# Two layers of attention: the transposes of normed heads and keys, issued 3, 4 and 2 steps later

## The chip, the cores and the metric
One core of a Trainium2 chip. The metric is the device time of one execution in microseconds (us). The kernel before takes 1375.31 us, the median of three runs (1373.74, 1375.31 and 1376.59).

## The reference
The program is a stack of three layers over 256 tokens of width 1024, in float32. The first (windowed attention beside a state-space layer, and a large product-key expert layer behind them) is not touched. The change lies in the last two, of which the reference is, in short:

```python
def even_layer(x, ...):
    h = rmsnorm(x, ln)
    aq, ak, av, az, bq, bk, bv, bz = split_cols(h @ w_in, EVEN_SPLITS)      # 8 x 512 columns
    oa = dilated_attention(rmsnorm(aq), rmsnorm(ak), av, slopes)            # 8 heads of 64
    ob = diff_attention(rmsnorm(bq), rmsnorm(bk), bv, lam, slopes)          # 4 pairs of heads
    return x + concat([oa * silu(az), rmsnorm(ob) * silu(bz)]) @ w_out

def odd_layer(x, ...):
    h = rmsnorm(x, ln)
    cq, ck, cv, cz, dq, dkc, dvc, dks, dvs, dkw, dvw, dz, dg = split_cols(h @ w_in, ODD_SPLITS)
    oc = moba_attention(rmsnorm(cq), rmsnorm(ck), cv, slopes)
    k_cmp = rmsnorm(compress_blocks(dkc, ...))
    v_cmp = compress_blocks(dvc, ...)
    od = nsa_attention(rmsnorm(dq), k_cmp, v_cmp, rmsnorm(dks), dvs, rmsnorm(dkw), dvw, sigmoid(dg), slopes)
    return x + concat([oc * silu(cz), od * silu(dz)]) @ w_out
```

Each `rmsnorm` of a query or key works on one head of 64 values. At 256 tokens both attentions of a layer are causal and see all earlier tokens of their bands.

## The kernel before
Tokens lie on the 128 partitions, in two halves (`th` = 0, 1). `Layer.enter` transposes the input into `xH` and `xL`, a float32 number split into a rounded part and the rest. A projection is a `group`: 512 output columns, two PSUM banks (one a half, of four banks with the tag `pr`), and eight chunks `k` of the 1024 inputs. For one chunk and one half `mm3` issues three matmuls (L1702 to L1704). So a step, one chunk for both halves, is six matmuls of 512 columns.

The weights come through `Feed`: a DMA of SyncE brings a unit of 128x1024 (two chunks), ScalarE rounds it to `H` (L102), and VectorE or GpSimd subtracts to get `Lo` (L103). In these layers of three units in a row GpSimd takes two and VectorE one. Units are cut three, later four, ahead of their use.

The order of the work is written by two generators. The background yields after each step of the projections; the foreground holds the attention and says how much background it lets by (`yield STEP`) or which mark it has to wait for (`yield "bk"`). `Flow.later(n, fn)` has `fn` issued after n further yields of the background. The order of the groups, eight steps each, is bq, bk, bv, aq, ak, av, bz, az in the even layer, and raw (the keys and values to be compressed and selected), windows (280 columns), dq, cq, ck, cv, dz, cz in the odd one. Eight steps of the output projection stand behind them, so the background has 72 steps. The framework's scheduler may slip ready instructions of the projections between those of the foreground.

At the end of a query or key group `Layer.heads` squares the result on ScalarE (L1192), reduces it on VectorE (L1193), takes an inverse root by thirteen small operations on VectorE (`rstd`, L1712 to L1720) and multiplies (L1196, L1197) into the buffers `qs`, of which there are four. Then it asks for `turn`: eight transposes on TensorE (L1203) into the PSUM banks with the tag `m` (three), copied out by ScalarE (L1206) or, where a gain is applied (bq, aq, cq), by VectorE (L1208), and a mark for the foreground. `windows` does the same for two keys: squares on GpSimd (L1469), one reduction (L1470), `rstd`, four products into `kn` (L1475), and the transposes of `kn` into `kT` (L1482), with the mark `kT`. On that mark the foreground starts `compress` (L1602 on), whose last part norms the compressed key `kr` (L1630) and transposes it (L1639) behind two steps of background. Scores follow (L1295, L1298), then the weights times the values (`weigh`, L1334 and L1340).

The last attention of a layer waits for the mark `az` (`cz`) of the eighth group ahead of its second half, and the output projection for `mixed01`, which the gate `bz` (`dz`) of the seventh group leads to.

Of the kernel before, what the change touches and what calls it, by code (L numbers as in the profile page):

```python
# [1106 lines left out]
def by_head(t):  # L1107
    return t.rearrange("p (h d) -> p h d", h=8)
# [6 lines left out]
STEP = 1280  # L1115
# [3 lines left out]
class Layer(Flow):  # L1119
# [63 lines left out]
    def heads(self, t, g, scale, mark):  # L1183

        c, nc, r = self.c, self.nc, self.r
        V = nc.vector

        def done(ps):
            ss = c.small.tile([128, 16], FT, tag="hss", name="hss")
            qs = [self.pool.tile([128, 512], FT, tag="qs", name="qs", bufs=4) for _ in range(2)]  # L1190
            for th in range(2):
                nc.scalar.activation(qs[th], ps[th], AF.Square, scale=r[:, th:th + 1])  # L1192
                V.tensor_reduce(ss[:, 8 * th:8 * th + 8], by_head(qs[th]), axis=AX.X, op=OP.add)  # L1193
            rr = c.rstd(ss, 16, 1.0 / 64)
            for th in range(2):
                V.tensor_scalar(ss[:, 8 * th:8 * th + 8], rr[:, 8 * th:8 * th + 8], r[:, th:th + 1], None, op0=OP.mult)  # L1196
                V.tensor_tensor(by_head(qs[th]), by_head(ps[th]), ss[:, 8 * th:8 * th + 8, None].to_broadcast([128, 8, 64]), op=OP.mult)  # L1197

            def turn():
                for th in range(2):  # L1200
                    p = c.psum("m")
                    for k in range(4):
                        nc.tensor.transpose(p[:, k * 128:(k + 1) * 128], qs[th][:, k * 128:(k + 1) * 128], c.ident)  # L1203
                    src, dst = p.rearrange("p (k t) -> p k t", k=4), t[:, :, th * 128:(th + 1) * 128]
                    if g is None:
                        nc.scalar.activation(dst, src, AF.Copy, scale=scale)  # L1206
                    else:
                        V.tensor_scalar(dst, src, g, scale, op0=OP.mult, op1=OP.mult)  # L1208
                self.mark(mark)
            self.later(5, turn)  # L1210
        return done

    def values(self, t, mark):
# [219 lines left out]
def odd(c, out):  # L1433
    nc, tc, A = c.nc, c.tc, c.A
    V, G = nc.vector, nc.gpsimd
    with tc.tile_pool(name="od", bufs=1, reuse_waits="tile") as pool:
        y = Layer(c, pool, "o")
# [19 lines left out]
        def windows(ps):  # L1457
            for th in range(2):
                nc.scalar.activation(kw[:, th].rearrange("p a b -> p (a b)"), ps[th][:, :256], AF.Copy, scale=y.r[:, th:th + 1])
                V.tensor_scalar(gt[:, th], ps[th][:, 256:280], y.r[:, th:th + 1], None, op0=OP.mult)  # L1460
            nc.scalar.activation(gt, gt, AF.Tanh, scale=0.5)
            V.tensor_scalar(gt, gt, 1.0, 0.5, op0=OP.add, op1=OP.mult)

            kss = pool.tile([128, 2, 2, 2], FT, name="kss")
            kn = pool.tile([128, 2, 2, 128], FT, name="kn")
            src = lambda z, th: raw[:, th, 256:384] if z == 0 else kw[:, th, 0]
            for z in range(2):
                for th in range(2):
                    G.tensor_tensor(kn[:, z, th], src(z, th), src(z, th), op=OP.mult)  # L1469
            V.tensor_reduce(kss.rearrange("p a b h -> p (a b h)"), kn.rearrange("p a b (h d) -> p (a b h) d", h=2), axis=AX.X, op=OP.add)  # L1470
            r = c.rstd(kss.rearrange("p a b h -> p (a b h)"), 8, 1.0 / 64)
            for z in range(2):
                for th in range(2):
                    n = 4 * z + 2 * th
                    V.tensor_tensor(kn[:, z, th].rearrange("p (h d) -> p h d", h=2), src(z, th).rearrange("p (h d) -> p h d", h=2),  # L1475
                                    r[:, n:n + 2, None].to_broadcast([128, 2, 64]), op=OP.mult)

            def turn():
                for z in range(2):
                    p = c.psum("m")  # L1480
                    for th in range(2):
                        nc.tensor.transpose(p[:, th * 128:(th + 1) * 128], kn[:, z, th], c.ident)  # L1482
                    nc.scalar.activation(kT[z][:, 16 - 16 * z:], p[:, :T], AF.Copy, scale=gg[:, 2 + z:3 + z])
                y.mark("kT")
            y.later(6, turn)

        y.background([y.group(y.values(raw, "raw"), first=True), y.group(windows, 280), y.group(y.heads(qd, None, 0.125, "dq")),
                      y.group(y.heads(qc, gg[:, 0:1], 0.125, "cq")), y.group(y.heads(kc, None, 1.0, "ck")), y.group(y.values(vc, "cv")),
                      y.group(y.swish(zd, lambda: y.meet("dz", gate_d))), y.group(y.swish(zc, lambda: y.mark("cz"))), y.out_first()])

        def fg():
# [7 lines left out]
            def ahead(i):  # L1499
# [17 lines left out]
                ready[i] = S, sc  # L1517

            yield from compress(y, XS, w1, gg, kT[0], vbd)
            yield "dq"  # L1520
            ready = {}
# [72 lines left out]
def compress(y, XS, w1, gg, kT, vbd):  # L1594

    c, nc, pool = y.c, y.nc, y.pool
    V = nc.vector
    ph = c.psum("m")
    for z in range(2):
        for n in range(16):  # L1600
            q = 32 * (n % 4)
            nc.tensor.matmul(ph[q:q + 32, z * 128:(z + 1) * 128], XS[z][:, n], w1[z][:, n * 128:(n + 1) * 128], start=(n < 4), stop=(n >= 12),  # L1602
                             tile_position=(0, q), skip_group_check=True)
    hp = pool.tile([128, 512], FT, tag="PT", name="hp", bufs=3)[:, :256]
    nc.scalar.copy(hp, ph[:, :256])
    yield STEP
    pt = c.psum("m")
    for z in range(2):
        nc.tensor.transpose(pt[:, z * 128:(z + 1) * 128], hp[:, z * 128:(z + 1) * 128], c.ident)
    hs = pool.tile([128, 2, 32], FT, name="hs")  # L1610
    V.tensor_reduce(hs, pt[:, :256].rearrange("p (z q n) -> p z n q", z=2, q=4), axis=AX.X, op=OP.add)
    h1 = pool.tile([128, 2, 2, 16], FT, name="h1")
    V.memset(h1, 0.0)
    for z in range(2):
        V.tensor_scalar(h1[:, z, :, 0:15], hs[:, z, 0:30].rearrange("p (k n) -> p k n", k=2), hs[:, z, 31:32], None, op0=OP.add)
    h2 = pool.tile([128, 2, 2, 16], FT, name="h2")
    nc.scalar.activation(h2, h1, AF.Tanh, scale=0.5)
    V.scalar_tensor_tensor(h2, h2, 1.0, h1, op0=OP.add, op1=OP.mult)
    V.tensor_scalar(h2, h2, 0.5, None, op0=OP.mult)
    yield STEP  # L1620
    w2 = lambda z: c.P2("phi2")[:, z * 64:(z + 1) * 64]
    p = c.psum("m")
    for k in range(2):
        nc.tensor.matmul(p[:16, k * 64:(k + 1) * 64], h2[:, 0, k], w2(0), start=True, stop=True)
    kr = pool.tile([16, 128], FT, name="kr")
    ks = pool.tile([16, 2], FT, name="ksc")
    nc.scalar.activation(kr, p[:16, :128], AF.Square)
    V.tensor_reduce(ks, kr.rearrange("p (k d) -> p k d", k=2), axis=AX.X, op=OP.add)
    r = c.rstd(ks, 2, 1.0 / 64, 16)
    V.tensor_tensor(kr.rearrange("p (k d) -> p k d", k=2), p[:16, :128].rearrange("p (k d) -> p k d", k=2),  # L1630
                    r[:, :, None].to_broadcast([16, 2, 64]), op=OP.mult)
    hr = pool.tile([128, 4, 2, 16], FT, name="hr")
    V.tensor_copy(hr, h2[:, 1, None].to_broadcast([128, 4, 2, 16]))
    p = c.psum("m")
    nc.tensor.matmul(p[:, :64], hr.rearrange("p r k n -> p (r k n)"), w2(1), start=True, stop=True)
    V.tensor_tensor(vbd, p[:, None, :64].to_broadcast([128, 8, 64]), c.cst("bd")[:, :, None].to_broadcast([128, 8, 64]), op=OP.mult)
    yield 2 * STEP
    p2 = c.psum("m")
    nc.tensor.transpose(p2[:, :16], kr, c.ident[:16, :16])  # L1639
    nc.scalar.activation(kT[:, :16], p2[:, :16], AF.Copy, scale=gg[:, 1:2])  # L1640
# [257 lines left out]
```

## Time and profile before
| | us |
|---|---|
| median of three runs | 1375.31 |
| the profiled execution | 1379.08 |
| its span (first to last instruction) | 1377.2 |
| TensorE busy in the span | 1283.5 (93%) |
| VectorE busy | 930.7 (68%) |
| ScalarE busy | 648.4 (47%) |
| GpSimd busy | 424.0 (31%) |
| mean granted clock of TensorE | 0.958 |

The profile is of one execution; times count from the start of its span. PE is TensorE, DVE VectorE, ACT ScalarE, POOL GpSimd. The last two layers begin at about 1012 us. [...] In a timeline, the bracket at the end of a row is the idle time of the engine just ahead of it and what ended it.

### The profile page before, as it was taken

The numbers are of one execution on the slowest core, as the hardware profiler recorded it, in microseconds if no ns is written. First come the engines' busy times: TensorE is split into PE (matmuls) and PEld (weight loads), VectorE is DVE, ScalarE is ACT, GpSimd is POOL, SyncE is SP. The second block draws the span as 40 slices with busy tenths as digits, with TensorE's granted clock in tenths as the row PEclk, the third lists the DMA queues.
The fourth block names the chain that finished last, engine by engine and source line by source line (L and its number), as shares of the span: only waits on it lengthen the run. The fifth ranks groups of instructions, "written<-read, shape, count | busy, mean of one in ns | idle before, by whom it ended". The sixth has DMA issues, their size and how long they took to land.

```text
span 1377.2 us, 21248 instructions
## 1 busy us (share of the span) xinstructions
PE 1283.5 (93%) x7816; PEld 1107.7 (80%) x7816; DVE 930.7 (68%) x2137; ACT 648.4 (47%) x1119; POOL 424.0 (31%) x257
## 2 busy tenths in 40 slices
PE   4569899999999999998999999999998989979998
PEld 4455789999999999998887888888876768756777
DVE  6963469898898666664788855555567845585734
ACT  4424345544545444444544444544554545533552
POOL 7010000477788777600000000000043426431143
PEclk9877989999999999999999999999999979997999
DMA  5359255788887777897999865665664325551231
GB/s 200 61 61 369 76 185 174 207 229 220 234 221 209 194 208 200 250 368 245 300 305 309 301 192 188 186 193 187 186 219 131 123 79 166 196 164 50 77 107 61
DMA packets 106296, 262.75 MB, mean 191 GB/s; under 512 B 31552, under 2 KB 37056, under 8 KB 103888
## 3 DMA queue, kind: packets, MB, share of 16 engines
q1 hardware_dynamic: 75280, 227.77, 52.9%
q0 software_dynamic: 21696, 16.85, 6.6%
q10 hardware_dynamic: 9216, 16.78, 3.3%
q8 instruction: 61, 1.00, 0.3%
q14 instruction: 43, 0.35, 0.1%
HBM read 232.72 MB, written 28.38 MB: 190 GB/s over the span
## 4 chain that ended last, share of the span: by engine, by line
PE 74%; DVE 11%; DMA 6%; issue 2%; ACT 1%; SPq 0%; DVEq 0%; ACTq 0%
PE ps L890 22%; PE ps L1702 10%; PE ps L1703 10%; PE ps L1704 10%; PE pr L1702 4%; PE pr L1704 4%; PE pr L1703 4%; PE m L1295 2%; DVE Lo L103 2%; DMA glu<-in_glu 2%; PE ps L1103 2%; DMA ga<-ascr 2%; PE o L1340 1%; DMA T<-kdr 1%; DVE rs L1719 1%
## 5 line engine op out<-in xcount | busy, mean ns | idle before, releaser
L102 ACT CAST H<-w 128x1024 fp32r<-128x1024 f32 (+1 forms) x370 | 386.0, 1045 | 502.4 <-PE ps L1703 211.5
L103 DVE TENSOR_TENSOR Lo<-w,H 128x1024 fp32r<-128x1024 f32 x310 | 386.0, 1246 | 171.8 <-ACT H L102 171.7
L103 POOL TENSOR_TENSOR Lo<-w,H 128x1024 fp32r<-128x1024 f32 (+1 forms) x60 | 141.8, 2367 | 626.2 <-ACT H L102 619.5
L1061 POOL DMA_INDIRECT wscr<-sent x128 | 241.0, 1883 | 225.8 <-DVE act L1038 157.0
L1702 PE MATMUL ps<-xH,H 128*128 128x256 f32 x1024 | 290.8, 284 | 0.0
L1703 PE MATMUL ps<-xL,H 128*128 128x256 f32 x1024 | 287.8, 281 | 0.0
L1704 PE MATMUL ps<-xH,Lo 128*128 128x256 f32 x1024 | 287.6, 281 | 0.0
L890 PE MATMUL ps<-H,a 128*128 128x512 f32 x1024 | 281.8, 397 | 5.3 <-ACT a L902 3.0
L890 PEld LDWEIGHTS ps<-H,a 128*128 128x128 f32 x1024 | 194.0, 190 | 51.3 <-ACT a L902 3.2
L1702 PEld LDWEIGHTS ps<-xH,H 128*128 128x128 f32 x1024 | 193.1, 189 | 0.0
L1703 PEld LDWEIGHTS ps<-xL,H 128*128 128x128 f32 x1024 | 193.1, 189 | 0.0
L1704 PEld LDWEIGHTS ps<-xH,Lo 128*128 128x128 f32 x1024 | 193.0, 188 | 0.0
L890 PE MATMUL ps<-Lo,a 128*128 128x512 f32 x512 | 161.7, 397 | 0.9 <-DVE Lo L103 0.9
L890 PEld LDWEIGHTS ps<-Lo,a 128*128 128x128 f32 x512 | 96.8, 189 | 24.5 <-DVE Lo L103 1.9
L900 DVE TENSOR_TENSOR act<-ga,act 128x256 f32<-128x256 f32 x128 | 47.4, 420 | 26.0 <-DMA ga<-ascr 25.8
L1702 PE MATMUL pr<-H,exH 128*128 128x512 f32 x128 | 54.3, 425 | 0.9 <-ACT exH L1143 0.9
L1702 PE MATMUL pr<-H,oxH 128*128 128x512 f32 (+1 forms) x128 | 52.9, 416 | 1.1 <-ACT oxH L1143 1.1
L903 DVE TENSOR_TENSOR a<-act,a 128x256 fp32r<-128x256 f32 x128 | 53.5, 419 | 0.0
L902 ACT CAST a<-act 128x256 fp32r<-128x256 f32 x128 | 51.3, 401 | 3.1 <-DMA ascr<-ga 2.1
L1704 PE MATMUL pr<-H,oxL 128*128 128x512 f32 (+1 forms) x128 | 52.6, 411 | 0.0
L1704 PE MATMUL pr<-H,exL 128*128 128x512 f32 x128 | 52.5, 410 | 0.0
L1703 PE MATMUL pr<-Lo,oxH 128*128 128x512 f32 (+1 forms) x128 | 51.9, 406 | 0.4 <-DVE Lo L103 0.4
(493 smaller groups left out, 1956.7 us busy)
## 6 DMA issues: line engine op xcount, KB each, us to landing
w<-in_ut SPq DMA_DIRECT2D x128, 512.0 KB, 4.4
w<-in_pv SPq DMA_DIRECT2D x128, 512.0 KB, 4.3
ascr<-ga ACTq DMA_DIRECT2D x64, 256.0 KB, 3.0
ga<-ascr SPq DMA_DIRECT2D x64, 256.0 KB, 5.5
w<-in_we SPq DMA_DIRECT2D x32, 512.0 KB, 3.6
w<-in_wod SPq DMA_DIRECT2D x28, 512.0 KB, 3.7
wscr<-zero POOLq DMA_DIRECT2D x4, 2048.0 KB, 30.3
w<-in_wqy SPq DMA_DIRECT2D x16, 512.0 KB, 3.5
```

The lines of the kernel that those rows point to most:

```text
L102: self.last = self.nc.scalar.copy(H, self.loaded[u])
L103: eng.tensor_sub(Lo, self.loaded[u], H.bitcast(FT))
L890: nc.tensor.matmul(acc[2 * th + n], a[:, s], b[:, n * 512:(n + 1) * 512], start=first and e == 0, stop=last and e == 2)
L900: V.tensor_tensor(src, ga[:, blk % 2], src, op=OP.mult)
L902: copied = nc.scalar.copy(aH, src)
L903: V.tensor_sub(aL, src, aH.bitcast(FT))
L1061: ins = c.nc.gpsimd.indirect_dma_start(out=c.wscr.rearrange("i b (t o) -> (i b t) o", o=1), out_offset=bass.IndirectOffsetOnAxis(ap=t.bitc ...
L1103: nc.tensor.matmul(p[:, a * 128:(a + 1) * 128], o1[:, a], o2[:, a], start=True, stop=True)
L1295: nc.tensor.matmul(sp[:, :off + nk], q(h)[:, ts], k(h)[:, :off + nk], start=True, stop=True)
L1702: nc.tensor.matmul(o, ah, bh, start=first, stop=False)
L1703: nc.tensor.matmul(o, ah, bl, start=False, stop=False)
L1704: nc.tensor.matmul(o, al, bh, start=False, stop=last)
```

## The change
The delay of `turn` in `heads` is eight yields instead of five (seven groups: bq, bk, aq, ak, dq, cq, ck); that in `windows` is ten instead of six; `compress` lets four steps by instead of two ahead of the transposes of `kr`. Nothing else differs.

```diff
@@ heads
                 self.mark(mark)
-            self.later(5, turn)
+            self.later(8, turn)
         return done
@@ windows
                 y.mark("kT")
-            y.later(6, turn)
+            y.later(10, turn)
@@ compress
     V.tensor_tensor(vbd, p[:, None, :64].to_broadcast([128, 8, 64]), ...)
-    yield 2 * STEP
+    yield 4 * STEP
     p2 = c.psum("m")
     nc.tensor.transpose(p2[:, :16], kr, c.ident[:16, :16])
```

In steps of the background the marks move so: `bk` from 21 to 24, `ak` from 45 to 48, `kT` from 22 to 26, `dq` from 29 to 32, `ck` from 45 to 48.

## Rows read from the trace of the kernel before
**Rows 1.** Waits of TensorE from 950 us on: total, times, longest.
```profile
PE m L1203 <- DVE qs L1197: 10.5, 3, 6.7
PE m L1482 <- DVE kn L1475: 5.4, 1, 5.4
PE m L1639 <- DVE kr L1630: 3.7, 1, 3.7
PE m L1334 <- DVE S L1402: 2.0, 1, 2.0
```
**Rows 2.** Timeline of TensorE: start, duration, line, operation, tiles, count, idle before.
```profile
1042.12 0.40 PE L1702 MATMUL pr<-H,exH 128*128 128x512 f32 x1
...
1048.87 0.39 PE L1704 MATMUL pr<-H,exL 128*128 128x512 f32 x1
1052.81 1.94 PE L1203 MATMUL m<-cstt,qs 128*128 128x128 f32 x8 [3.56 <-DVE qs L1197]
...
1108.58 1.94 PE L1203 MATMUL m<-cstt,qs 128*128 128x128 f32 x8 [6.69 <-DVE qs L1197]
...
1219.07 1.16 PE L1482 MATMUL m<-cstt,kn 128*128 128x128 f32 x4 [5.39 <-DVE kn L1475]
...
1239.09 0.20 PE L1639 MATMUL m<-cstt,kr 16*128 16x16 f32 x1 [3.73 <-DVE kr L1630]
```
**Rows 3.** Windows of 8 us: busy time by engine, granted clock, DMA share, GB/s.
```profile
1048.00:1056.00 8.00, 4.44 (x20) 3.26 (x18) 5.15 (x10) 2.21 (x3) 2.98 (x2) 0.79 0.47 141
...
1072.00:1080.00 8.00, 5.97 (x35) 4.91 (x34) 7.69 (x17) 3.68 (x5) 3.47 (x2) 1.00 0.50 154
...
1096.00:1104.00 8.00, 5.89 (x26) 4.44 (x24) 7.69 (x17) 2.69 (x3) 4.66 (x2) 1.00 0.34 131
1104.00:1112.00 8.00, 3.42 (x14) 2.68 (x14) 4.98 (x21) 1.19 (x2) 0.08 (x1) 0.69 0.56 197
1112.00:1120.00 8.00, 8.00 (x28) 5.46 (x28) 3.12 (x23) 4.00 (x17) 0.00 (x0) 0.50 0.00 1
1120.00:1128.00 8.00, 8.00 (x31) 5.86 (x30) 3.35 (x14) 4.35 (x18) 0.00 (x0) 0.74 0.23 68
...
1216.00:1224.00 8.00, 4.93 (x70) 4.08 (x71) 4.52 (x12) 1.31 (x3) 1.46 (x1) 0.57 0.51 147
...
1240.00:1248.00 8.00, 8.00 (x27) 4.43 (x25) 2.40 (x21) 2.05 (x3) 2.35 (x1) 0.51 0.07 13
1248.00:1256.00 8.00, 8.00 (x21) 4.69 (x21) 3.04 (x23) 3.38 (x17) 0.00 (x0) 0.50 0.16 58
1256.00:1264.00 8.00, 8.00 (x31) 6.45 (x31) 5.51 (x30) 4.71 (x19) 0.00 (x0) 0.71 0.01 2
```
**Rows 4.** Timeline of VectorE from the copy of `bq` to the heads of `bk`.
```profile
1039.80 1.40 DVE L1208 TENSOR_SCALAR qk<-m,gq 128x512 f32<-128x512 f32 x2
1042.34 1.38 DVE L1193 TENSOR_REDUCE hss<-qs 128x8 f32<-128x512 f32 x2 [1.15 <-ACT qs L1192]
...
1046.05 0.18 DVE L1718 TENSOR_TENSOR rs<-rs 128x16 f32<-128x16 f32 x1
1046.26 2.41 DVE L1719 TENSOR_TENSOR rs<-rs 128x16 f32<-128x16 f32 x1
...
1051.98 1.28 DVE L1197 TENSOR_TENSOR qs<-pr,hss 128x512 f32<-128x512 f32 x2
```
**Rows 5.** Timeline of GpSimd in the same stretch.
```profile
1046.24 2.40 POOL L103 TENSOR_TENSOR Lo<-w,H 128x1024 fp32r<-128x1024 f32 x1 [3.14 <-ACT H L102]
```
**Rows 6.** Timeline of ScalarE, the squares of `ak`.
```profile
1094.26 1.39 ACT L1192 ACTIVATE qs<-pr,r 128x512 f32<-128x512 f32 x2 [1.00 <-PE pr L1704]
```
**Rows 7.** Timeline of VectorE, their reduction.
```profile
1101.76 1.26 DVE L1193 TENSOR_REDUCE hss<-qs 128x8 f32<-128x512 f32 x2
```
**Rows 8.** Timeline of VectorE behind the products `kn`.
```profile
1225.35 0.42 DVE L1611 TENSOR_REDUCE hs<-m 128x64 f32<-128x256 f32 x1 [4.59 <-PE m L1609]
```
**Rows 9.** The page's costliest groups: VectorE's share of the Lo tiles.
```profile
L103 DVE TENSOR_TENSOR Lo<-w,H 128x1024 fp32r<-128x1024 f32 x310 | 386.0, 1246 | 171.8 <-ACT H L102 171.7
```

## The prediction
> **What bounds the kernel now.** I read the page first. The span is 1377.2 us; the change touches only the last two layers, which begin near 1012 us. There the waits of TensorE come next, because its share of busy time is an average and the lost time has to be found place by place. The reader sees that three of its four longest groups of waits are transposes waiting for VectorE [rows 1]: 10.5 us for the normed heads (`qs`), 5.4 us for the window keys (`kn`), 3.7 us for the compressed key (`kr`), 19.6 us in all. The timeline of TensorE gives the places [rows 2]: 3.56 us ahead of the transposes of `bk`, 6.69 us at `ak`, 5.39 us at `kT`, 3.73 us at `kr` (with the transposes of `dq` right behind it); the missing 0.2 us is at `bq`. [...]
>
> **The price of a step.** A step of the projections is two blocks of three matmuls. The thirty matmuls from 1042.12 to 1048.87 us [rows 2] start 6.75/29 = 0.233 us apart, and they are exactly the five steps of today's delay. A step is 1.40 us, three steps 4.2 us, four steps 5.6 us. No instruction is added or taken away: 24 steps lie between the transposes of `bk` and `ak` before (21st to 45th) and after (24th to 48th), and the ends are held by other marks: in both layers the last half of the attention waits for the gate `az`/`cz` at step 64, later than everything that moves. So the change is worth what it takes off stalls and slow clock, and nothing else. The DMA queue sees the same weights in the same order, only earlier where TensorE stalls less; it is given no new wait.
>
> **bk.** TensorE arrives at 1052.81 - 3.56 = 1049.25 us and would arrive at about 1053.4 us. The transposes of `bq` (eight) now stand behind the end of the `bk` group instead of five steps into it; they only change places. The normed heads need from the reduction at 1042.34 to 1051.98 plus half of 1.28 = 1052.6 us [rows 4]. This is a chain of small operations of 0.18 us, of which two took 2.4 us, each beside a Lo of GpSimd (2.40 us) [rows 5]. Three more steps consume one and a half more weight units, two thirds of whose Lo tiles are GpSimd's, so about one more such block of 2.2 us may fall into the chain; the copy of `bq` on VectorE comes ahead of it as well. I take 0.6 us as the stall that is left: 3.0 us gained, with bounds of 3.56 (none left) and -1.8 (below, the slower rival). The clock deficit of 0.21 x 8 = 1.7 us in that window [rows 3] goes with it in part: 1.0 us, bounds 0 and 1.7.
>
> [...]
>
> **ak.** Here more steps do not help by themselves. ScalarE has the squares of `ak` from 1094.26, but VectorE begins to reduce them at 1101.76 us [rows 6, 7], because it is still at the norms of the foreground: it is busy 7.69 of 8 us from 1072 to 1104 (first and last of four windows, the others 7.5 and 7.8) [rows 3]. Foreground and `ak` both shift by three steps, so the queue ahead of `ak` has the same contents, measured from `bk`. I leave the stall of 6.69 us as it is and take 0.5 us; bounds 0 and 4.2 plus a clock deficit of (0.31 + 0.50 + 0.26) x 8 = 8.6 us.
>
> **kT.** TensorE arrives at 1219.07 - 5.39 = 1213.68 and would arrive at 1219.3 us, when `kn` is ready today. Four more steps eat two more weight units, and the squares and reductions of `dq` begin ahead of the turn now. Most of one more block by GpSimd falls in: 1.7 us of stall left, 3.7 us gained, bounds 5.39 and -1.6. Of the clock deficit of 0.43 x 8 = 3.4 us I take 1.0, since a good part of that window is idle anyway; bounds 0 and 3.4.
>
> **kr and dq.** The two are ready almost together now, the transposes of both start right after 1239 us [rows 2], since their chains alternate on VectorE. In the change `dq` ends its projection two steps ahead of `kT`, not two behind it, so its chain of about 6 us can use the 4.59 us in which VectorE idles up to 1225.35 [rows 8], and `kr` has VectorE more to itself. Against this fewer steps lie between `kT` and `dq`: 26th to 32nd, against 22nd to 29th. I take 2.5 of the 3.73 us, bounds 0 and 3.73.
>
> **The clock behind it.** From 1240 to 1264 us the deficit is (0.49 + 0.50 + 0.29) x 8 = 10.2 us [rows 3], though TensorE is busy all the time; VectorE needs 2.40 + 3.04 + 5.51 = 10.95 of these 24 us, so it leaves room. But the scores are handed to VectorE through three PSUM banks, and what follows keeps VectorE nearly full. Of a stall that shrinks to 1.2 us I expect the clock to survive about as often as not: I take 1.5 us, bounds 0 and 10.2.
>
> **The sum.** 3.0 + 1.0 + 0.5 + 3.7 + 1.0 + 2.5 + 1.5 = 13.2 us. Against the profiled execution: 1377.2 - 13.2 = 1364.0 us of span, 1.9 us around it, 1365.9 us. That execution (1379.08) was 3.8 us over the median of the three runs (1375.31), so the forecast for a median is 1375.3 - 13.2 = 1362.1 us.
>
> What is late next: the projections have four PSUM banks, two a group, and the banks of a `heads` group are read until `qs` is written. The group after next needs them at the ninth step. So behind a turn at eight steps the same chain would stop TensorE at the same place; a longer delay could gain nothing.
>
> **Rivals.**
> 1. *VectorE is the bound all along.* The stalls only change places: what is saved at `bk` and `kT` comes back at `ak`, `kr` or at the transposes of the weights `S`. For it: 7.69 of 8 us busy [rows 3]. Against it: three steps of matmuls stand ahead of the turn that stood behind it, and they fill a stall wherever it is; VectorE idles 4.59 us at the one place where its load moves to [rows 8]. Time: what remains is 1 us, 1374 us.
> 2. *Slower.* Place: the three chains on VectorE. Each gets the work of the steps that move ahead of it: at `bk` the copy of `bq` (1.40 us) [rows 4] and two GpSimd blocks of 2.3 us, 6.0 us for 4.2 us of steps; at `kT` the reductions of `dq` (1.4), two blocks and a Lo of VectorE (1.2) [rows 9], 7.2 us for 5.6 us. Each stall grows by 1.6 to 1.8 us, 3.4 us, and the slow clock stays: 1378.7 us. It decides from the point at which the chain from the first reduction to `qs` is longer than 10.3 + 4.2 = 14.5 us at `bk`. Against it: two blocks are in today's chains already, and GpSimd's Lo tiles come at the pace of the steps, about one in two steps.
> 3. *Everything goes.* The stalls of `bk`, `kT` and `kr` vanish, that of `ak` shrinks by 4.2 us, and the clock stays up behind three of them: 12.7 + 4.2 + half of the deficits (1.7 + 3.4 + 10.2)/2 = 7.6, together 24.5 us, 1351 us.
>
> **How the numbers follow.** What a measurement can tell from no change is about 0.2%, 2.75 us. The forecast's case (a gain of 4 to 20 us) has 0.66, the third rival (over 20 us) 0.12, the first 0.13, the second 0.09. Faster is 0.66 + 0.12 and a small part of the first rival, 0.79; within 0.2% 0.12; slower 0.09. The range of 1352 to 1372 us holds the forecast's case with the better part of the third rival's, and leaves out the second and most of the first.
>
> **What would show it.** Right: in the waits of TensorE those for `qs` fall from 10.5 to about 7.5 us with `ak` as nearly all of it, `kn` from 5.4 to under 2, `kr` from 3.7 to about 1; the granted clock in the 8 us behind `bk` is 1.00. Wrong: a stall at `bk` over 2 us, or a chain there longer than 12 us with more than two blocked operations (then the blocks by GpSimd decide), a stall at `ak` well under 6 us (then VectorE had slack and I undersold it), or new waits of the same size at the transposes of `S` or at the first matmul of a projection (then VectorE was the bound).

## The result, and the profile after

The changed kernel takes 1355.49 us, the median of four runs (1350.70 to 1366.05), beside 1375.95 us of four runs of the kernel before: a ratio of 0.9851, 95% interval 0.9803 to 0.9899. Timed a second time on another chip it was 0.9859 (0.9823 to 0.9895). The forecast was 1362.1 us, 13.2 us less than before; the medians lie 20.5 us apart.

The profiled execution is the shortest of the four, 1350.70 us with a span of 1348.6. Of the 28.6 us between the two spans, 6.0 lie ahead of the two layers, where nothing was changed. So the layers are compared by themselves, the even one from the first transposes of its input to the first matmul of the odd layer's projections, the odd one from there to the end. The windows of the kernel before (first fence) and of the changed one (second) have, behind the bounds, the length, the busy times of TensorE, its weight loads, VectorE, ScalarE and GpSimd, and the granted clock of TensorE (a share of its full speed):

```profile
1011.10:1183.30 172.20, 154.59 (x721) 121.03 (x719) 111.35 (x268) 86.14 (x163) 75.12 (x34) 0.93 0.41 129
1183.30:1377.20 193.90, 178.32 (x932) 137.01 (x932) 117.08 (x378) 87.04 (x198) 65.39 (x34) 0.93 0.35 113
```
```profile
1005.10:1162.63 157.53, 146.48 (x720) 114.66 (x718) 112.25 (x268) 85.95 (x163) 78.73 (x34) 1.00 0.44 141
1162.63:1348.60 185.97, 170.86 (x932) 133.48 (x932) 121.50 (x378) 87.26 (x198) 65.27 (x34) 0.97 0.36 118
```

The even layer became 14.7 us shorter and the odd one 7.9. The same instructions keep TensorE busy 15.6 us less, by the clock; its idle time (length less busy time) fell by 7.0 us. The two layers differ in this: in the even one the idle time fell from 17.6 to 11.1 us and the busy time by 8.1, in the odd one the idle time only from 15.6 to 15.1 us and the busy time by 7.5.

Not all of the 14.7 us is the change's. In the first 16 us of the even layer, ahead of anything that moved, the mean clock was 0.89 in the profile before (1011.10 to 1027.10) and 1.00 in this one (1005.10 to 1021.10). The end of the `bk` group, where the next group's first matmul starts, comes 31.0 us into the layer before (1042.12) and 29.8 after (1034.91): 1.2 us are gained before the delays can tell.

TensorE's waits in the changed kernel (total, times, longest), which answer to [rows 1]:

```profile
PE m L1203 <- DVE qs L1197: 4.6, 2, 2.5
PE m L1334 <- DVE sc L1560: 3.0, 1, 3.0
...
PE m L1482 <- DVE kn L1475: 2.1, 1, 2.1
PE m L1295 <- DVE st L1298: 1.9, 2, 1.7
PE m L1624 <- issue: 1.7, 1, 1.7
...
PE m L1639 <- DVE kr L1630: 0.8, 1, 0.8
```

The old waits went from 19.6 to 7.5 us, and three new ones came in the odd layer (`sc`, `st` and the one at L1624), 6.6 us together. The places, against [rows 2] (`bk`, `aq`, `ak`, `kT`, `kr`, and the first transposes of weights):

```profile
1046.13 1.04 PE L1203 MATMUL m<-cstt,qs 128*128 128x128 f32 x8
1083.16 1.32 PE L1203 MATMUL m<-cstt,qs 128*128 128x128 f32 x8 [2.14 <-DVE qs L1197]
1098.11 1.23 PE L1203 MATMUL m<-cstt,qs 128*128 128x128 f32 x8 [2.49 <-DVE qs L1197]
1200.76 0.94 PE L1482 MATMUL m<-cstt,kn 128*128 128x128 f32 x4 [2.10 <-DVE kn L1475]
1218.05 0.20 PE L1639 MATMUL m<-cstt,kr 16*128 16x16 f32 x1 [0.78 <-DVE kr L1630]
1237.48 0.48 PE L1334 MATMUL m<-cstt,sc 128*128 128x128 f32 x1 [2.96 <-DVE sc L1560]
```

The stall at `bk` is gone, that at `ak` is 2.49 us, and `aq`, which had none, has 2.14. The granted clock behind `ak`, `kT` and the wait for `sc` (windows of 8 us, against [rows 3]):

```profile
1104.00:1112.00 8.00, 7.91 (x39) 6.00 (x39) 3.49 (x20) 7.22 (x32) 0.00 (x0) 1.00 0.23 68
...
1200.00:1208.00 8.00, 7.24 (x82) 5.89 (x83) 7.50 (x27) 1.25 (x3) 0.00 (x0) 0.79 0.55 190
...
1232.00:1240.00 8.00, 5.04 (x23) 4.14 (x22) 7.15 (x24) 3.50 (x14) 2.25 (x1) 0.78 0.53 140
1240.00:1248.00 8.00, 8.00 (x37) 6.11 (x36) 4.01 (x18) 3.67 (x9) 2.35 (x1) 0.79 0.22 66
```

All of the even layer is at 1.00, and the long stretch at 0.50 behind `kr` is gone. The chain of `bk` on VectorE (from the first reduction to the normed heads), against [rows 4], has two blocked operations as before, that is small ones that take over 2 us instead of 0.17:

```profile
1034.34 0.69 DVE L1193 TENSOR_REDUCE hss<-qs 128x8 f32<-128x512 f32 x1 [0.93 <-ACT qs L1192]
1034.94 1.40 DVE L1208 TENSOR_SCALAR qk<-m,gq 128x512 f32<-128x512 f32 x2
...
1039.23 2.30 DVE L1718 TENSOR_TENSOR rs<-rs 128x16 f32<-128x16 f32 x1
...
1041.99 2.38 DVE L1718 TENSOR_TENSOR rs<-rs 128x16 f32<-128x16 f32 x1
...
1045.11 1.28 DVE L1197 TENSOR_TENSOR qs<-pr,hss 128x512 f32<-128x512 f32 x2
```

From 1034.34 to 1045.75 (half of the last row) it takes 11.4 us, 1.1 us longer than before, for the copy of `bq` now stands inside it. That and the old stall are 4.7 us, more than the 4.2 us of the added steps; the rest is covered by the eight transposes of `bq` (0.8 us from 1034.12), which now stand behind the end of the group, where the chain has already begun.

### The profile page after: what moved, and what is told of

The parts are those of the page before. It is cut to its first block, busy times and chain, and to the rows that moved or that the text cites. A ratio compares the mean times of both kernels' runs of the same rounds, so it can differ in the third digit from the quotient of the medians.

```text
span 1348.6 us, 21243 instructions
## 1 busy us (share of the span) xinstructions
PE 1263.5 (94%) x7816; PEld 1092.7 (81%) x7816; DVE 936.7 (69%) x2137; ACT 648.5 (48%) x1119; POOL 423.5 (31%) x257
## 4 chain that ended last, share of the span: by engine, by line
PE 74%; DVE 10%; DMA 7%; issue 2%; ACT 1%; SPq 0%; DVEq 0%; ACTq 0%
PE ps L890 20%; PE ps L1702 10%; PE ps L1703 10%; PE ps L1704 10%; PE pr L1702 4%; PE pr L1704 4%; PE pr L1703 4%; DMA ga<-ascr 3%; DMA glu<-in_glu 2%; PE ps L1103 2%; DVE Lo L103 2%; PE m L1295 2%; PE o L1340 2%; DMA T<-kdr 1%; DVE act L900 1%
## 5 line engine op out<-in xcount | busy, mean ns | idle before, releaser
L103 POOL TENSOR_TENSOR Lo<-w,H 128x1024 fp32r<-128x1024 f32 (+1 forms) x60 | 145.3, 2427 | 608.5 <-ACT H L102 582.2
L1061 POOL DMA_INDIRECT wscr<-sent x128 | 237.6, 1856 | 213.0 <-DVE act L1038 151.0
L1090 DVE TENSOR_TENSOR o<-cstt,sel 128x512 f32<-128x512 f32 x32 | 22.1, 691 | 43.0 <-PE ps L1103 27.6
L844 ACT ACTIVATE ga<-ps 128x256 f32<-128x256 f32 x128 | 48.4, 378 | 6.4 <-PE ps L1704 5.5
```

Source lines behind the costliest of these rows:

```text
L103: eng.tensor_sub(Lo, self.loaded[u], H.bitcast(FT))
L844: nc.scalar.activation(ga[:, blk % 2], p[:, :T], AF.Gelu)
L1061: ins = c.nc.gpsimd.indirect_dma_start(out=c.wscr.rearrange("i b (t o) -> (i b t) o", o=1), out_offset=bass.IndirectOffsetOnAxis(ap=t.bitc ...
```

## Experiments

Ratios are to the kernel before on the same chip, with 95% intervals; "even" and "odd" are the layers' times in us in the profiled execution (172.2 and 193.9 before). Where an edit doesn't touch a layer, its time shows what such a time can tell: even 171.0, 170.9 and 170.9 (e2, e5, e6), odd 194.0 and 192.4 (e4, e3).

**e1, the heads alone**
```diff
-            self.later(5, turn)
+            self.later(8, turn)
```


> Only the delay of the heads is changed (5 to 8); kT and kr stay at 6 and 2 steps. Theory A (stalls add up, each delay pays at its own place): the even layer is as in the full change, about 14.7 us shorter (172.2 to 157.5 us), the odd one keeps the stall of 5.4 us at kT and about 4 us at kr or dq, so 1359 to 1363 us. Rival B (the chain on VectorE simply moves the stall on): the gain of the even layer stays under 6 us, 1370 us or more.


1367.22 us, 0.9918 (0.9892 to 0.9945); even 159.3, odd 193.2. The time is 4 us over theory A's range, of which 3.4 go with the chip (1378.74 us before on it). The layers came as A has them: the heads bring the even layer's gain and nothing in the odd one, where `kn` keeps its 5.4 us.

**e2, kT and kr alone**
```diff
-            y.later(6, turn)
+            y.later(10, turn)
-    yield 2 * STEP
+    yield 4 * STEP
```


> Only kT (6 to 10 steps) and kr (2 to 4) are changed, heads stay at 5. Theory A: the even layer keeps its stalls of 3.6 and 6.7 us and its slow clock, the odd one gains most of its 7.9 us: 1367 to 1371 us. Rival B: dq at 5 steps now comes ahead of kT in the code and waits behind the norm of the window keys on VectorE, the stall at kT (5.4 us) turns into one at dq of the same size: 1374 to 1377 us.


1371.09 us, 0.9952 (0.9924 to 0.9981); even 171.0, odd 185.3, all of the odd layer's gain. B falls. The gains of e1 and e2, 0.8% and 0.5%, add up to that of the whole change within their intervals.

**e3 and e4, one group of heads each**
```diff
-            self.later(5, turn)
+            self.later(8 if mark in ('bk',) else 5, turn)
```


> Only bk is delayed by 8 steps, all else stays at 5, 6 and 2. The foreground starts three steps later, but ak does not follow: 21 steps between them instead of 24. Theory Q (VectorE's queue decides, ak waits for the norms of the foreground): the stall of 3.6 us at bk goes and that at ak grows from 6.7 to 9 to 11 us, with the clock behind it at half: 1374 to 1377 us. Theory A (each delay pays at its own place): 5 us gained, 1370 to 1372 us.


1382.62 us, 1.0029 (1.0002 to 1.0056), even 173.1: no gain, as Q says, though not in the way. (The profiled execution, 1373.96 us, was the shortest of twelve.) The stall at `ak` did not grow; a new one came up at `aq`:

```profile
1048.89 1.04 PE L1203 MATMUL m<-cstt,qs 128*128 128x128 f32 x8
1083.77 1.94 PE L1203 MATMUL m<-cstt,qs 128*128 128x128 f32 x8 [5.62 <-DVE qs L1197]
1104.79 1.94 PE L1203 MATMUL m<-cstt,qs 128*128 128x128 f32 x8 [6.59 <-DVE qs L1197]
```
e4 has `('ak',)` in that line.


> Only ak is delayed by 8 steps. The stall at bk stays at 3.6 us with its slow clock of some 5 us. Theory Q: the queue ahead of ak is as before, so its stall falls by the three steps, 6.7 to about 2.5 us, and behind it the granted clock stays near 1.00 as it does behind 2.0 us now: 4.2 us and up to 8.6 us of clock deficit, 1364 to 1371 us. Rival C (the clock falls behind any stall over 2 us): only the 4.2 us, 1371 us.


1369.54 us, 0.9944 (0.9918 to 0.997), even 162.6: 9.6 us from `ak` alone in the profiled execution, again the shortest of twelve (1360.80 us); by the ratio it is some 8 us. So Q. Part of the stall only moved to a wait for a Lo tile eleven matmuls earlier, but the clock of the layer is 0.98 instead of 0.93:

```profile
1002.30:1164.94 162.64, 149.19 (x721) 116.74 (x719) 112.88 (x268) 86.39 (x163) 75.37 (x34) 0.98 0.43 136
```
```profile
1097.34 0.50 PE L1703 MATMUL pr<-Lo,exH 128*128 128x512 f32 x1 [2.25 <-DVE Lo L103]
...
1100.40 1.23 PE L1203 MATMUL m<-cstt,qs 128*128 128x128 f32 x8 [0.23 <-DVE qs L1197]
```

**e5 and e6, kT and kr one by one**
```diff
-            y.later(6, turn)
+            y.later(10, turn)
```


> Only kT is delayed (6 to 10 steps); kr stays at 2 steps, heads at 5. Theory A (the delay of kT carries the odd layer's gain): the stall at kT is about 2 us as with both, the odd layer 186 to 189 us (193.9 before, 185.3 with kT and kr), 1368 to 1372 us. Rival D (kr is needed too: it is two steps nearer to its chain and takes the stall over, 4 us or more): the odd layer 191 us or more, over 1373 us.


1376.62 us, 0.9987 (0.9949 to 1.0025), odd 192.4.
```diff
-    yield 2 * STEP
+    yield 4 * STEP
```


> Only kr is delayed (2 to 4 steps). Theory A: kT keeps its stall of 5.4 us; kr comes together with or behind dq as before, its chain on VectorE is unchanged, so the stall of 3.7 us moves to dq or shrinks by less than 1 us; odd layer 192 to 194 us, 1375 to 1379 us. Rival D: the stall of 3.7 us goes and with it half of the slow clock behind it (10.2 us of deficit), odd layer 186 to 188 us.


1377.4 us, 0.9987 (0.9962 to 1.0012), odd 193.6, stalls as before. e6 is as A has it; in e5 D has the time but not the cause, since no stall came up at `kr`. Alone they bring 1.5 and 0.3 us, together 8.6 (e2). The odd layer of e5 (first fence) and of e2 (second):

```profile
1183.05:1375.40 192.35, 180.15 (x932) 138.02 (x932) 119.07 (x378) 87.30 (x198) 65.44 (x34) 0.94 0.35 114
```
```profile
1193.23:1378.50 185.27, 170.62 (x932) 132.97 (x932) 117.93 (x378) 87.44 (x198) 65.47 (x34) 0.98 0.37 119
```

e5 has less idle time (192.35 - 180.15 = 12.2 us against 14.7) and is slower: the whole difference is clock. It is lost later, in the scores of `dq`:

```profile
1255.00:1263.00 8.00, 6.96 (x26) 4.30 (x26) 7.61 (x29) 0.53 (x2) 4.28 (x2) 0.80 0.69 196
1263.00:1271.00 8.00, 8.00 (x16) 4.23 (x16) 3.23 (x15) 1.19 (x2) 0.00 (x0) 0.50 0.00 1
1271.00:1279.00 8.00, 8.00 (x42) 6.00 (x40) 4.81 (x13) 5.58 (x20) 0.00 (x0) 0.85 0.23 66
```

TensorE had idled only 1.0 us in the first of these windows (8.00 - 6.96); why the clock fell in e5 and not in e2 stays open.

**e7, heads at twelve steps** (the changed kernel with 12 for 8)


> The changed kernel with the delay of the heads at 12 instead of 8. Theory P (the projection of the group after next needs the two PSUM banks that the heads are read from, at the ninth step): the stalls of 2.1 and 2.5 us at aq and ak reappear as waits of the same size at the first matmul of a projection; layers within 1.5 us of those of the changed kernel (157.5 and 186.0 us). Rival A (any further delay pays until its stall is gone): the even layer 153 to 155 us.


1369.3 us, 0.9928 (0.9898 to 0.9958); even 166.6, odd 195.4. The bank decides as P says, for TensorE waits at the first matmul of a projection:

```profile
1089.44 0.50 PE L1702 MATMUL pr<-H,exH 128*128 128x512 f32 x1 [3.73 <-DVE qs L1197]
```
But P's 1.5 us are missed by far: each layer is 9 us slower than in the changed kernel (6.0 and 8.6 against its second profile, e11), at clocks of 0.93 and 0.92. The waits for `qs` add up to less than in the changed kernel (3.7 against 4.6 us); what grew is TensorE's busy time (156.2 and 182.6 against 146.5 and 170.9). Why the clock is lower here is not shown.

**e8, the kernel before with all Lo tiles of the two layers on VectorE**
```diff
-        LE = [P, P, V]
+        LE = [V]
```


> The kernel before with all Lo tiles of the two layers on VectorE (1.25 us each) and none on GpSimd, delays as before. Theory L (the chains are long because each Lo of GpSimd blocks a small operation of VectorE by some 2.2 us, against 1.2 us for doing the Lo itself): the chain of bk is about 2 us shorter, the stalls at bk, ak and kT shrink by 1 to 3 us each and the clock recovers: 1362 to 1372 us. Rival V (VectorE is full, more work on it delays every chain): stalls grow, 1380 to 1390 us.


1336.0 us, 0.9669 (0.9632 to 0.9707): 42.4 us less than the kernel before on the same chip (1378.41), about twice the change's gain, with no delay touched. L was right, and too careful; V is out.

```profile
1014.70:1165.22 150.52, 146.48 (x720) 114.48 (x718) 112.97 (x297) 85.98 (x163) 6.50 (x4) 1.00 0.50 150
1165.22:1336.80 171.58, 165.28 (x932) 129.36 (x932) 120.66 (x403) 87.51 (x198) 8.09 (x8) 1.00 0.39 125
```

VectorE does 29 instructions more in the even layer, at 1.21 us each 35 us of added work, and is busy 113.0 instead of 111.4 us. So the same other work took it some 33 us less: that much of its busy time before was waiting. Its chain of `bk`, and TensorE behind it:

```profile
1043.62 1.38 DVE L1193 TENSOR_REDUCE hss<-qs 128x8 f32<-128x512 f32 x2 [0.51 <-ACT qs L1192]
...
1047.63 1.22 DVE L103 TENSOR_TENSOR Lo<-w,H 128x1024 fp32r<-128x1024 f32 x1
...
1049.87 1.28 DVE L1197 TENSOR_TENSOR qs<-pr,hss 128x512 f32<-128x512 f32 x2
```
```profile
1050.70 0.63 PE L1203 MATMUL m<-cstt,qs 128*128 128x128 f32 x4 [0.19 <-DVE qs L1197]
```

6.9 us to the first heads (1050.5) instead of 10.3, with two Lo tiles of its own inside (the one shown and one at 1045.35) and no operation of the norm over 0.18 us, and five steps are enough. The moved Lo tiles are also ready sooner (1.21 us instead of 2.40), but that is not where the gain lies: TensorE waited for a Lo tile once in both layers before, 0.4 us.

**e9 and e10, the changed kernel with other engines for Lo**
```diff
-        LE = [P, P, V]
+        LE = [V]
```


> The changed kernel with all Lo tiles of the two layers on VectorE. Theory L (both edits buy the same thing, slack against the blocks by GpSimd): with the blocks gone the chains fit into five and six steps, so the longer delays gain nothing more; layers within 2 us of 150.5 and 171.6 us (the kernel before with Lo on VectorE), 1334 to 1338 us. Theory A (the delays pay on their own): 3 us or more less, 1333 us or less.


1329.69 us, 0.9647 (0.9583 to 0.9711); even 149.6, odd 172.5, together 322.1 as in e8. The time lies in A's range, but on another chip than e8's; the ratio, whose interval overlaps e8's, doesn't part the two, and the layers' times say L: with the blocks gone the longer delays buy nothing there.
e10 has `LE = [P, V]`.


> The changed kernel with every second Lo tile on GpSimd instead of two of three. Theory L: the gain follows the number of blocks: a quarter of GpSimd's Lo tiles gone, of the 20 us between the changed kernel and 1336 us some 5 us, 1348 to 1352 us. Rival C (the stalls are now small enough that only the clock decides): nothing between, either 1355 us or 1338 us.


1356.09 us, 0.9814 (0.976 to 0.9869); even 156.9, odd 188.7, together 345.6 against 343.5 and 347.4 in two profiles of the changed kernel. L's 5 us were not found in the layers' times: with 21 Lo tiles on GpSimd instead of 30 in the even layer, `ak` still waits 2.8 us. The ratio leaves room for them (0.9814 beside 0.9851 and 0.9859, the intervals overlap). C's number fits, and which of the Lo tiles count for the chains stays open.

**e11, the changed kernel once more**


> The changed kernel once more. If the layers' times are a matter of order and blocks alone, they repeat within 1 us (157.5 and 186.0 us) and what varies is the untouched first 1000 us. Rival C (stalls of 2 to 3 us lie at the edge at which the clock falls): even or odd layer 4 us or more off, with a mean granted clock in it that is lower by 0.02 or more. Ratio 0.983 to 0.988.


1359.82 us, 0.9859 (0.9823 to 0.9895); even 160.6, odd 186.8. The odd layer repeats within 1 us. The even one is 3.1 us off, a little less than C's four, at a mean clock of 0.97 instead of 1.00. The stalls at `aq` and `ak` are the same 2.14 and 2.49 us. About half of the 3.1 us is lost ahead of both: the transposes of `aq` come 79.7 us into the layer instead of 78.1, and the clock of the first 16 us was 0.79 (1015.40 to 1031.40) instead of 1.00. The other half comes behind `ak`, where this time the clock fell.

```profile
1015.40:1176.01 160.61, 150.08 (x720) 117.35 (x719) 111.94 (x268) 86.08 (x163) 78.68 (x34) 0.97 0.41 138
```
```profile
1110.02 1.64 PE L1203 MATMUL m<-cstt,qs 128*128 128x128 f32 x8 [2.49 <-DVE qs L1197]
```
```profile
1112.00:1120.00 8.00, 7.91 (x39) 4.85 (x38) 4.78 (x32) 4.42 (x18) 2.36 (x1) 0.87 0.42 132
```

**e12, the changed kernel with all Lo tiles on GpSimd** (`LE = [P]`)


> The changed kernel with all Lo tiles of the two layers on GpSimd. Theory L: half as many blocks again of 2.2 us each, against 1.25 us of VectorE saved for each Lo moved; stalls at the transposes grow again although VectorE has less work: 1368 to 1385 us. Rival V (VectorE's own work is the load): faster than the changed kernel, 1345 to 1352 us.


1386.56 us, 1.0063 (1.0037 to 1.0089), slower than the kernel before and 2.0% over the changed one on the same chip (1359.82); even 172.3, odd 201.7. L, just over its range: VectorE has twelve Lo tiles less in the even layer, about 15 us at 1.21, is busy only 5.4 us less (106.9), and the stalls are back.

```profile
1113.65 1.94 PE L1203 MATMUL m<-cstt,qs 128*128 128x128 f32 x8 [6.24 <-DVE qs L1197]
...
1226.73 1.11 PE L1482 MATMUL m<-cstt,kn 128*128 128x128 f32 x4 [7.40 <-DVE kn L1475]
```

## Why the prediction was right, and where it was not

The forecast's sign and range held: the waits for `qs`, `kn` and `kr` and the slow clock behind them (0.79 behind `bk`, 0.50 to 0.57 behind `ak`, `kT` and `kr` [rows 3]) were where the time lay. The size, 13.2 us, was two thirds of the measured 20.5, and the gain was not made up as forecast. The forecast's gains by term, beside the two profiles (a deficit is the time in a stretch that the missing clock stands for):

| term | forecast, us | measured |
|---|---|---|
| `bk`, stall | 3.0 | 3.6 (3.56 to none) |
| clock behind it | 1.0 | deficit 1.7 to 0 |
| `ak`, all | 0.5 | stall 4.2 less, `aq` 2.1 more, `S` 1.6 less; clock deficit 8.6 to 0 |
| even layer | 4.5 | 14.7, of it 1.2 ahead of the delays |
| `kT`, stall | 3.7 | 3.3 |
| its clock | 1.0 | window 0.57 to 0.79 |
| `kr` | 2.5 | 3.0 |
| clock behind `kr` | 1.5 | no long stretch at 0.5, new waits of 6.6 |
| odd layer | 8.7 | 7.9 |

**The step that failed is `ak`.** I held that its stall stays since the queue ahead of it has the same contents measured from `bk`. The stall fell from 6.69 to 2.49 us. The contents are the same, but the queue was not full all the way. From the transposes of `bk` to those of `ak` VectorE was busy 44.6 of 55.8 us before and 44.0 of 52.0 after (the fourth number is its busy time):

```profile
1052.81:1108.58 55.77, 46.96 (x228) 36.95 (x229) 44.58 (x131) 27.20 (x57) 19.15 (x8) 0.96 0.33 104
1046.13:1098.11 51.98, 46.54 (x230) 35.78 (x228) 43.98 (x131) 27.73 (x59) 21.99 (x8) 1.00 0.39 129
```

The four full windows that I read are preceded by 20 us in which it also waited, for TensorE among others (6.2 of the 20 us), whose granted clock was 0.79 in the first of these windows, 1048:1056 [rows 3], and 1.00 in the next two. Its idle time between the two fell from 11.2 to 8.0 us, and the way from `bk` to `ak` is 3.8 us shorter. It isn't shorter with one of the two marks moved, 55.9 us in e3 and 56.1 in e4, and it is again in e1 (53.1) and e11 (52.0), where all heads move; what shortens it, the clock, the later `aq` or the order of the blocks, the runs don't part. e3 and e4 do show that `bk` and `ak` were not two terms to be added: with `bk` alone delayed nothing is gained and 5.6 us of waiting come up at `aq`, and `ak` alone gains 9.6 us. At `aq`, which the forecast did not price, 2.1 us of waiting came up in the changed kernel too.

**The clock was the larger half of the even layer.** I priced what lies behind `ak` at nothing. The layer's mean clock went from 0.93 to 1.00, and TensorE's busy time fell by 8.1 of the 14.7 us. e11 shows that this is no sure gain: at the same stalls the layer was 3 us longer, by a lower clock at its start and behind `ak`. So part of the 14.7 us is luck of that execution.

**The odd layer's number, 8.7 for 7.9, is luck in part.** The forecast had 6.2 us of stalls and 2.5 of clock in it. The stalls of `kT` and `kr` did shrink by 6.2 us, but the new waits take as much, so TensorE idles only 0.5 us less; 7.5 of the 7.9 us are its busy time, the clock. The first rival was right that the stalls change places there, and wrong that the time is then not gained. Nor were `kT` and `kr` two terms to be added: alone they bring 1.5 and 0.3 us, together 8.6 (e5, e6, e2).

**Right:** the stalls of `bk`, `kT` and `kr` within 0.6 us each; one more block by GpSimd in the chain of `kT`, the third, with 2.1 us of stall left where 1.7 were said:

```profile
1197.61 2.37 DVE L1718 TENSOR_TENSOR rs<-rs 128x8 f32<-128x8 f32 x1
```
```profile
1197.59 2.36 POOL L103 TENSOR_TENSOR Lo<-w,H 128x1024 fp32r<-128x1024 f32 x1 [0.65 <-ACT H L102]
```

Right, too, that the end of a layer is held by other marks (from the transposes at L1240 to the end of the even layer it is 38.1 us in both kernels, from 1145.18 and from 1124.51), and that a delay beyond eight steps runs into the PSUM banks (at twelve TensorE waited 3.73 us for `qs` at the first matmul of a projection, e7). Of the slower rival one half is true, the chain of `bk` did grow by the copy of `bq`, but by 1.1 us and without a further block.

Of the signs that the prediction named, the clock of 1.00 behind `bk` and the 0.8 us at `kr` came as said, and `kn` just missed (2.1 us, under 2 said). Two of its signs of being wrong came up: `ak` well under 6 us, and new waits in the odd layer, the longest ahead of the transposes of the weights (`sc`, 2.96 us).

**What was not asked.** The prediction priced the blocks as a risk to the change. They were the cause of the stalls: e8 takes them away, the waits for `qs` fall from 10.5 to 0.6 us, and it gains twice what the delays do; in e9 the delays add nothing to it in the two layers, and in e12 more blocks bring the stalls back although VectorE has less to do. The delays are slack against a chain that need not be so long. The best two versions are these, 0.9669 and 0.9647 of the kernel before.

## What to carry to other kernels

A busy share of VectorE can be waiting, as some 33 us of it were here in the even layer (e8): where GpSimd works at the same time, look for operations of one shape with two durations (0.17 and over 2 us here), and count what the engine would need alone before giving it slack or taking work away from it. Stalls along one queue were not terms to be added (e3 to e6); follow the queue from one to the next, back to where the engine last idled. And what the stalls of TensorE cost here was its idle time plus what the clock took behind them, which was twice as much (15.6 us of busy time against 7.0 of idle time) and varied from run to run (a mean clock of 1.00 and of 0.97 in the even layer of the same kernel).

## What the runs showed of the hardware

Small VectorE operations of `rstd`, 0.17 us elsewhere, that began within 0.2 us of a GpSimd subtraction of 2.40 us took 2.2 to 2.4 us in both profiles, with two inputs (L1718, L1719) as with one (L1712, L1713, L1714). Moving the subtractions to VectorE halved their time (2.40 to 1.21 us) and raised its busy time by 1.6 us in the even layer and 3.6 in the odd one (e8). GpSimd's own time grew too: its pairs of Lo took 4.8 us at five places of the changed kernel and 5.7, 6.2 and 6.2 at 1005.8, 1065.6 and 1088.4 us, where a Lo of VectorE ran within the pair (at 1006.66, 1065.97 and 1090.18). Without GpSimd's subtractions in the two layers the time was 3.3% below the kernel before (e8), with all of them on GpSimd 0.6% above it (e12, which has the longer delays besides; against the changed kernel it is +2.0%).

The granted clock behind a stall was not a matter of the stall's length alone: 2.49 us at `ak` was followed by 1.00 in one execution and 0.87 in another, and in e5 a stretch with 1.0 us of idle time by 0.50. Over whole executions time goes with the mean clock: the four of the changed kernel were 1350.70, 1351.31, 1359.67 and 1366.05 us at 0.976, 0.972, 0.966 and 0.959.
